# Issuing the first load of x as two transfers: 32 rows of x, then 224

## The chip, the core and the metric

The kernel runs on one core of one Trainium2 chip. A core has engines that run side by side and wait for each other through semaphores: TensorE (PE, matrix products into the accumulation memory PSUM; its weight loads are listed as PEld), VectorE (DVE), ScalarE (ACT), GpSimd (POOL) and SyncE (SP), which here only issues DMA transfers. All transfers run on the core's 16 DMA engines. The metric is the time of one execution on the device in microseconds (us). The kernel before takes 358.84 us, the median of three runs between 358.75 and 359.02 us.

## The reference

```python
batch, seq, hidden = 16, 512, 768          # x: 16 x 512 x 768, w_qkv: 768 x 2304, float32
qkv = np.matmul(x, w_qkv)
q, k, v = qkv[..., :768], qkv[..., 768:1536], qkv[..., 1536:]
return np.stack([q, k, v], axis=0)         # 3 x 16 x 512 x 768, float32
```

It is one matrix product: 8192 rows of x (25 MB) by 2304 columns of weights (7 MB), and the 75 MB result is stored as three blocks.

## The kernel before

The rows of x are worked through in 32 pairs of 128-row blocks; "pair p" is rows 256p to 256p + 255. The 2304 columns are cut into two groups of 1024 (number q = 0 and 1) and a rest of 256. In the long main part, each pair and column group is multiplied by a seven-product scheme (Strassen-like, with sums of quarter blocks of x, made by GpSimd or VectorE, and sums of quarter blocks of the weights, made once by VectorE). Pairs are read in 32-partition pieces there and turned by VectorE. The order of the instructions on every engine is the order of the program text; nothing reorders it.

The start is different, since no weights are there yet. Pairs 0 and 1 are multiplied plainly, in bf16, while the weights arrive. What matters for the change is all in this start:

- All loads of the start are issued by SP, in this order: pair 0 of x (`load_rows(0)`, L453, 768 KB), pair 1 of x (`load_rows(1)`, L456, 768 KB), six pieces of the first weight block of 256 KB each (`load_blocks(0, 0, 1)`, L457), two halves of the second weight block (768 KB each), and then pair 2 of x in eight pieces of 96 KB, with the weights of the rest between them.
- `load_rows` (L159) puts rows m and 128 + m of a pair into partition m of the tile xin: 128 partitions, two runs of 3072 bytes in each. It is one transfer of 256 runs.
- The first eight transfers are issued at once. From the ninth on, each transfer on SP waits for the landing of the one issued eight before it, because eight completion semaphores are used in turn.
- `busy(10)` (L538) gives PE ten products of a zero tile, with nothing to wait for but the zeroing of that tile.
- `cast_rows(0)` (L539) turns pair 0 into bf16: VectorE takes one half of the columns (L165), ScalarE the other (L166), for each of the two 128-row blocks. These instructions wait for the landing of pair 0.
- `turn_rows(0, ...)` (L540) has PE transpose pair 0, 12 transposes of 128x128 (L185); VectorE and ScalarE copy them back from PSUM into xb (L194, L192). Between the two kinds of copies stands `cast_rows(1)`, which waits for the landing of pair 1.
- VectorE then casts the first two weight pieces (L542 and L543, recorded as L476), and `turn_rows(1)` (L544) transposes pair 1.
- `block(0, 0, ...)` (L547) are the first real products, 24 of 128x512 at L496, weight piece by weight piece. In PE's order they stand behind the 12 transposes of pair 1.

Of the kernel before, what the change touches and what calls it, by code (L numbers as in the profile page):

```python
# [10 lines left out]
def kernel(  # L11
# [20 lines left out]
    nc = tc.nc  # L32
    P = 128
# [87 lines left out]
    xin, xf, xb, sr = {}, {}, {}, {}  # L121
# [34 lines left out]

    def load_rows(p):  # L159
        xin[p] = xin_pool.tile([P, 2, K], fp32, name="xin")  # L160
        rows = x_flat[p * 2 * P:(p + 1) * 2 * P, :]
        nc.sync.dma_start(xin[p][:], rows.rearrange("(r m) k -> m r k", m=P))  # L162

    def copy_halves(dst, src):
        nc.vector.tensor_copy(out=dst[0], in_=src[0])  # L165
# [284 lines left out]
    ND = 2  # L450
    zero = xb_pool.tile([P, CB], bf16, name="zero", tag="xb")
    nc.vector.memset(zero[:], 0.0)
    load_rows(0)  # L453
    nc.scalar.activation(tiny[:], zero[:, :1], ident)
    make_identity(nc, eye)
    load_rows(1)  # L456
    load_blocks(0, 0, 1)  # L457
    load_blocks(0, 1)
# [246 lines left out]
```

## Time and profile before

| what | value |
|---|---|
| median of three runs | 358.84 us |
| the profiled execution: its own time, its span | 358.81 us, 357.0 us |
| PE busy (matmul), share of the span | 350.6 us, 98% |
| VectorE, ScalarE, GpSimd busy | 74%, 52%, 50% |
| DMA: bytes moved, mean rate | 108.10 MB, 303 GB/s |
| issue of the first two loads of x on SP | 0.74 to 1.69 us |
| start of the casts of pair 0, of pair 1 | 4.97 us, 6.93 us |
| first real product on PE | 8.29 us |

The span is the time between the first and the last recorded event of the one profiled execution; 1.8 us of its own time lie outside it. Times in the profile count from the start of the span. A busy PE is not proof of a PE at its peak: the records overlap and their ends are modelled. How late PE gets its first real product, and whether it waits later, is read from the chain of waits and from the timeline.

The trace also holds a record of each DMA packet (start, duration, size; one packet is one contiguous run of a transfer here) and of each landing: every transfer counts its semaphore up 16 times, once for each DMA engine, and is complete with the sixteenth.

### The profile page before, as it was taken

What the parts mean: (1) busy time and instruction counts of PE and PEld (TensorE: products, weight loads), DVE (VectorE), ACT (ScalarE), POOL (GpSimd) and SP (SyncE); (2) the same over time, 40 slices, a digit from 0 to 9 for tenths busy, and PEclk for the clock granted to TensorE, in tenths of its full rate; (3) what the DMA queues carried; (4) which work ended last, traced back from release to release, by engine and by line L of the source; (5) the groups of instructions that cost most, each with busy time, mean ns of one, the idle gap of its engine ahead of it and who ended that gap; (6) DMA issues with size and microseconds to landing.
All of it is one profiled execution on the core that took longest, in us unless ns stands there. A gap on an engine that the chain in (4) does not pass through costs nothing.

```text
span 357.0 us, 5315 instructions
## 1 busy us (share of the span) xinstructions
PE 350.6 (98%) x1757; PEld 252.1 (71%) x1776; DVE 264.4 (74%) x310; ACT 185.0 (52%) x317; POOL 177.3 (50%) x184
## 2 busy tenths in 40 slices
PE   7999999999999999999999999999999999999996
PEld 3474677768677686877768677686877768677674
DVE  3789876796877869777695877869777695876743
ACT  4587754545454553645545454553645545454553
POOL 0031773376566453665535566353665535566320
PEclk9999999999999999999999999999999999999999
DMA  7997999999999898998979899698999979887497
GB/s 296 380 353 238 325 378 340 373 317 348 308 311 340 257 361 206 347 266 285 361 197 385 227 342 307 209 402 213 347 263 307 331 196 392 225 303 280 155 380 260
DMA packets 82075, 108.10 MB, mean 303 GB/s; under 512 B 4992, under 2 KB 62080, under 8 KB 82048
## 3 DMA queue, kind: packets, MB, share of 16 engines
q1 hardware_dynamic: 75088, 102.52, 85.7%
q10 hardware_dynamic: 6960, 5.24, 5.5%
q8 instruction: 14, 0.23, 0.3%
q14 instruction: 13, 0.11, 0.1%
HBM read 32.24 MB, written 75.50 MB: 302 GB/s over the span
## 4 chain that ended last, share of the span: by engine, by line
PE 74%; POOL 15%; DVE 6%; issue 3%; DMA 2%; ACT 0%; SPq 0%
PE ps L258 56%; PE ps L321 12%; PE ps L496 6%; DVE xf L155 6%; POOL xb L205 5%; POOL s L226 3%; POOL s L225 3%; POOL s L227 3%; DMA xin<-in_x_dram 2%; PE ps L185 0%; DVE o L304 0%; ACT xc L166 0%; SPq L162 0%; DVE orem L424 0%; ACT orem L423 0%
## 5 line engine op out<-in xcount | busy, mean ns | idle before, releaser
L258 PE MATMUL ps<-t,s 128*128 128x512 f32 x720 | 177.9, 395 | 0.0
L258 PEld LDWEIGHTS ps<-t,s 128*128 128x128 f32 x720 | 135.1, 188 | 29.5
L155 DVE STREAM_TRANSPOSE xf<-xin 128x768 f32<-128x768 f32 (+1 forms) x45 | 93.3, 2075 | 4.3 <-DMA xin<-in_x_dram 4.3
L258 PE MATMUL ps<-b,xb 128*128 128x512 bf16 x343 | 81.6, 379 | 1.1
L298 DVE TENSOR_TENSOR o<-o,ps 128x512 f32<-128x512 f32 x56 | 38.5, 688 | 50.7 <-ACT o L297 50.0
L205 POOL CAST xb<-xf 128x1536 bf16<-128x1536 f32 x28 | 41.1, 1467 | 56.9 <-DVE xf L155 54.8
L225 POOL TENSOR_TENSOR s<-xf 128x384 fp32r<-128x384 f32 x29 | 31.0, 1068 | 72.9 <-DVE xf L155 71.1
L258 PEld LDWEIGHTS <-xb 128*128 128x128 bf16 x360 | 33.9, 98 | 36.7 <-issue 3.9
L304 DVE TENSOR_TENSOR o<-o,ps 128x512 f32<-128x512 f32 x60 | 41.1, 687 | 20.5 <-PE ps L258 19.4
L297 ACT ACTIVATE o<-ps 128x512 f32<-128x512 f32 x56 | 33.5, 598 | 42.1 <-PE ps L258 42.1
L258 PE MATMUL ps<-b,s 128*128 128x512 f32 x180 | 50.6, 389 | 0.0
L301 ACT ACTIVATE o<-ps 128x512 f32<-128x512 f32 x60 | 35.9, 598 | 25.2 <-PE ps L258 22.8
L378 DVE TENSOR_TENSOR o<-o,ps 128x512 f32<-128x512 f32 x78 | 47.8, 680 | 0.0
L321 PE MATMUL ps<-w_rem,xb 128*128 128x256 bf16 x384 | 47.4, 273 | 0.0
L286 ACT ACTIVATE o<-ps 128x512 f32<-128x512 f32 x60 | 35.9, 599 | 19.4 <-PE ps L258 14.0
L321 PEld LDWEIGHTS <-xb 128*128 128x128 bf16 x384 | 37.3, 98 | 11.5 <-issue 0.5
L335 ACT ACTIVATE orem<-ps 128x512 f32<-128x512 f32 x31 | 18.5, 598 | 48.3 <-PE ps L321 34.0
L258 PEld LDWEIGHTS ps<-b,s 128*128 128x128 f32 x180 | 33.8, 188 | 7.0
L226 POOL TENSOR_TENSOR s<-s,xf 128x384 fp32r<-128x384 f32 x29 | 29.5, 1018 | 2.3
L227 POOL TENSOR_TENSOR s<-xf 128x384 fp32r<-128x384 f32 x29 | 29.4, 1015 | 0.0
L229 POOL TENSOR_TENSOR s<-xf,s 128x384 fp32r<-128x384 f32 x29 | 29.2, 1008 | 0.0
L382 ACT ACTIVATE o<-ps 128x512 f32<-128x512 f32 x26 | 15.5, 598 | 17.9 <-PE ps L258 17.3
(49 smaller groups left out, 161.2 us busy)
## 6 DMA issues: line engine op xcount, KB each, us to landing
out_dram<-o SPq DMA_DIRECT2D x60, 768.0 KB, 4.6
out_dram<-o SPq DMA_DIRECT2D x75, 256.0 KB, 3.8
xin<-in_x_dram SPq DMA_DIRECT2D x88, 192.0 KB, 5.6
out_dram<-orem SPq DMA_DIRECT2D x31, 256.0 KB, 2.2
xin<-in_x_dram ACTq DMA_DIRECT2D x24, 192.0 KB, 4.4
st<-in_w_qkv_dram SPq DMA_DIRECT2D x5, 768.0 KB, 7.9
xin<-in_x_dram SPq DMA_DIRECT2D x2, 768.0 KB, 4.9
st<-in_w_qkv_dram SPq DMA_DIRECT2D x6, 256.0 KB, 6.0
```

Source lines behind the costliest of these rows:

```text
L155: nc.vector.transpose(turned[:, g:g + n], rows[:, g:g + n])
L205: nc.gpsimd.tensor_copy(out=xb[p][:], in_=xf[p][:])
L225: 1: lambda g: g.tensor_tensor(s[:, 1], a21, a22, op=add),
L226: 2: lambda g: g.tensor_tensor(s[:, 2], s[:, 1], a11, op=sub),
L227: 3: lambda g: g.tensor_tensor(s[:, 3], a11, a21, op=sub),
L258: nc.tensor.matmul(ps[:], lhs[j], rhs[j], start=(start and j == 0), stop=(j == KH - 1), skip_group_check=True,)
L286: nc.scalar.activation(c12, u.x[:], ident)
L298: nc.vector.tensor_tensor(c22, c22, u.y[:], op=add)
L301: nc.scalar.activation(c21, u.x[:], ident)
L304: nc.vector.tensor_tensor(c12, c12, u.y[:], op=add)
L321: nc.tensor.matmul(ps, xb[p][:, j, r * P:(r + 1) * P], w_rem[j // KH][:, j % KH, :], start=(j == 0), stop=(j == KT - 1), skip_group_check= ...
L378: dve.tensor_tensor(c, c, u.z[:], op=add)
```

## The change

The helper `load_rows` gets a list of partition ranges and issues one transfer for each of them. Pair 0 of x is loaded with two ranges, partitions 0 to 15 and then 16 to 127. As each partition holds two rows, that is 32 rows (96 KB, 32 runs of 3072 bytes) and 224 rows (672 KB, 224 runs). Pair 1 is loaded as before, in one transfer. Nothing is changed on the engines that compute: the casts of pair 0 stand where they stood and now wait for two landings. SP issues one transfer more, ahead of all that follow.

```diff
-    def load_rows(p):
+    def load_rows(p, parts=(slice(0, P), )):
         xin[p] = xin_pool.tile([P, 2, K], fp32, name="xin")
         rows = x_flat[p * 2 * P:(p + 1) * 2 * P, :]
-        nc.sync.dma_start(xin[p][:], rows.rearrange("(r m) k -> m r k", m=P))
+        rows = rows.rearrange("(r m) k -> m r k", m=P)
+        for m in parts:
+            nc.sync.dma_start(xin[p][m], rows[m])
...
-    load_rows(0)
+    load_rows(0, (slice(0, 16), slice(16, P)))
     nc.scalar.activation(tiny[:], zero[:, :1], ident)
     make_identity(nc, eye)
     load_rows(1)
```

## The prediction

> **What bounds the kernel now.** I read the chain that ended last first, in its opening 20 us (start, length, what):
>
> ```profile
> 0.74 0.44 SPq L162
> 1.18 0.06 issue
> 1.24 5.67 DMA xin<-in_x_dram
> 6.91 0.02 issue
> 6.93 0.53 ACT xc L166
> 7.46 0.05 issue
> 7.51 0.95 PE ps L185 x12
> 8.46 2.82 PE ps L496 x13
> ```
>
> The run waits for pair 1 of x until 6.91 us, then goes through a cast and PE's twelve transposes into the first real products. Then I asked who PE waits for over the whole span:
>
> ```profile
> PE ps L469 <- DVE zero L452: 1.2, 1, 1.2
> PE ps L185 <- ACT xc L166: 0.6, 1, 0.6
> ```
>
> That is the whole list: after the cast of pair 1, PE waits for nobody up to its last product. So the start shifts the end one for one, and the question is only when pair 1, and the weights right behind it, land. The timeline (start, duration, idle time before and what ended it) shows how tightly these follow the loads:
>
> ```profile
> 0.74 0.95 SPq L162 DMA_DIRECT2D xin<-in_x_dram  x2
> 4.97 0.63 DVE L165 CAST xc<-xin 128x384 bf16<-128x384 f32 x2 [3.84 <-DMA xin<-in_x_dram]
> 6.12 0.77 DVE L194 COPY xb<-ps 128x384 bf16<-128x384 bf16 x2 [0.52 <-PE ps L185]
> 6.93 0.63 DVE L165 CAST xc<-xin 128x384 bf16<-128x384 f32 x2
> 8.26 0.43 DVE L476 CAST b<-st 128x512 bf16<-128x512 f32 x1 [0.27 <-DMA st<-in_w_qkv_dram]
> ```
>
> Last, the rate of the DMA engines in short stretches (last two columns: busy share, GB/s):
>
> ```profile
> 1.75:2.00 0.25, 0.25 (x2) 0.00 (x0) 0.00 (x0) 0.25 (x1) 0.00 (x0) 1.00 1.13 172
> 2.00:2.25 0.25, 0.25 (x2) 0.15 (x1) 0.00 (x0) 0.22 (x2) 0.00 (x0) 1.00 0.59 98
> 2.25:2.50 0.25, 0.25 (x2) 0.06 (x1) 0.00 (x0) 0.00 (x0) 0.00 (x0) 1.00 0.32 86
> 2.50:2.75 0.25, 0.25 (x2) 0.09 (x1) 0.00 (x0) 0.00 (x0) 0.00 (x0) 1.00 0.81 209
> 3.00:3.25 0.25, 0.25 (x2) 0.02 (x1) 0.00 (x0) 0.00 (x0) 0.00 (x0) 1.00 1.00 406
> 9.00:10.00 1.00, 1.00 (x6) 0.48 (x5) 0.93 (x3) 0.86 (x2) 0.00 (x0) 1.00 1.04 402
> 15.00:16.00 1.00, 1.00 (x6) 0.49 (x5) 1.00 (x3) 1.00 (x3) 0.00 (x0) 1.00 1.07 373
> 17.00:18.00 1.00, 1.00 (x6) 0.43 (x5) 0.77 (x2) 0.49 (x2) 0.69 (x1) 1.00 1.14 275
> 18.00:19.00 1.00, 1.00 (x8) 0.59 (x7) 0.38 (x1) 0.78 (x2) 1.00 (x2) 1.00 1.20 249
> ```
>
> The reader is to see three things. The first packet starts 1.1 us after SP begins the issue (1.84 against 0.74 us). For about 0.9 us the engines then crawl: the packet records show first packets of 0.12 to 0.59 us where later ones of the same 3072 bytes take 0.121 us. From 3.0 us the queue is full and moves 400 GB/s, so nothing but bytes in front of pair 1 sets its landing. And at 17 to 19 us the rate falls to 249: there the 32-partition pieces of pair 2 run one behind another.
>
> **The change, part by part.**
>
> *One transfer more to issue.* The issues of the first loads take 0.44 to 0.45 us on SP with 0.05 between, so every later issue moves about 0.45 us back. Pair 1's goes from 1.24 to about 1.65, its packets could start near 2.75, and in the run of before its turn comes only at about 4.1 us (the first landing of pair 0, 4.45, less some 0.35 from the last packet of an engine to its landing record): over 1 us of cover. Without that cover it would cost 0.45. The weights behind are covered by still more. The queue of semaphores shifts by one, and each transfer keeps its partner eight before; new is only that the sixth weight piece, issued at 4.37 before and about 4.8 now, waits for the small first part, which lands near 3.1. Behind it on SP stand the second weight block and pair 2, with over 4 us of queued data ahead of them. Cost 0.
>
> *The small first part starts earlier.* Issues of 32-partition pieces that had waited take 0.31 us at least, such of 128 partitions 0.34 to 0.38. A shorter issue puts the first packet earlier by 0.03 to 0.13; I take 0.08, nearest to the difference between these rows. Gain −0.08.
>
> *What the first part does in the slow start.* It gives each engine two packets. In the run of before, each engine got through two or three packets until about 2.7 us. The lower bound is a gain: if the crawl comes from the first touch alone and the large part's packets find the path open at about 2.3 us (its issue near 1.2 plus 1.1), up to 0.4 us of crawl is saved. The upper bound: the 32-partition pieces take 0.396 us each (the landing records of six in a row, 17.65 to 20.03), 248 GB/s; half as many partitions at half that rate are 98,304 bytes in 0.79 us, all of it behind the first latency of about 0.45, ending near 3.0, so +0.3. I take 0: 0.79 from 1.76 ends at 2.55, inside the crawl.
>
> The page "SBUF — State Buffer" of the Trainium skill (section "Door 1: The DMA port swizzle") has partitions 0 to 15 reach only 4 of 16 ports, at a measured 104 GB/s; an estimate by it is 0.95 us for this part, ending at 2.71, and the sum would rise by about 0.1. No run here shows 16 partitions alone.
>
> *What the large part does.* 112 partitions over 16 engines is 7 each, 14 packets. At the full-height row (0.121 us a packet) that is 1.69 us, and the two parts together cost no more than before: lower bound 0. The other bound is from the 32-partition pieces: eight packets an engine at 0.036 us (their best in the trace, mixed with other traffic) would be 0.288 us, and they take 0.396, a factor of 1.37. By that factor the large part takes 2.32 us, +0.63. Pieces that do not cover the whole height make engines wait for each other at the writing side; with 7 partitions to an engine instead of 8 the engines' shares no longer coincide with those of the full-height transfers, so I go by the height-cut row although 112 is nearer to 128 in number: being cut is what sets it apart. Worse than the factor is possible where one engine meets others at each step, up to +1.1. I take +0.63. The slowest engine carries the lag through pair 1 and all weights, as each engine works its list in order at one rate.
>
> *Two waits on the cast of pair 0.* One more semaphore instruction, 0.02 to 0.05 us as in the rows of that kind on VectorE and PE. VectorE ends the copies of pair 0 at 6.894, just ahead of pair 1's landing at 6.905, so of 0.05 some 0.04 shows at most if pair 1 lands on time; with both loads late alike the same. I take +0.02.
>
> Sum: −0.08 + 0 + 0.63 + 0.02 = +0.57 us. The profiled execution's own time was 358.81 (357.0 of span and 1.8 around it), 0.03 under the median, so 359.38 by it and 359.41 by the median; I say 359.4. Pair 1 would land near 7.47, and the first real product start near 8.86.
>
> **The rivals.**
>
> *Hidden anyway.* The large part runs at the full rate and the early start cancels the second wait: −0.08 + 0.02, 358.8. For it: 112 is almost 128; the whole load is 16 packets an engine either way. Against it: the 249 GB/s at 18 us. The page "DMA: Bandwidth & Descriptors" (section "Rules for kernel authors") says of two transfers to disjoint partition halves: "Don't bother — they serialize"; by that rule the time stays here or rises a little. No run here shows it for a load cut in two.
>
> *The warm start, faster.* The small part takes the crawl on itself while the large one is being issued, and the large one runs at 400 GB/s from 2.3 to 2.4 us. Pair 1 then lands 0.3 to 0.5 us earlier: 358.4. For it: the crawl costs about 0.6 us (221 KB moved up to 3.0 us, where 406 GB/s from 1.84 on would have moved 471), and by far the longest packets are each engine's first two. It decides if the crawl is tied to the time of the first touch and not to each engine's first packets of each transfer, and if the height-cut part isn't slowed. Against it: in the records the third packet of most engines starts only at 2.65 to 2.95, later than a start of the large part at 2.3 would help much.
>
> *The first part is itself the brake.* Its writes come after the first latency, and the large part meets the worse sharing: +0.3 and +0.63 to +1.1, 359.8 to 360.2. For it: 16 partitions are half of the row that runs at 248 GB/s. Against it: the crawl leaves room.
>
> **How the numbers follow.** Forecast (height-cut large part, 359.0 to 359.8): 0.50. Hidden anyway: 0.20. Warm start: 0.13. The brake: 0.17. About 0.2%, 0.72 us, is what a measurement of this kernel tells from no change. Faster than 358.12 takes a saving of the whole crawl: 0.03, out of the warm start. Slower than 359.56: a third of the forecast's chance and nearly all of the brake's, 0.33. The rest, 0.64, is within. The range from 358.45 to 360.0 leaves out about half of the warm start and half of the brake, 0.15 together.
>
> **What would show it.** Right: pair 1's cast starts at 7.3 to 7.7 on ACT, the first product about 1.36 later, the rate is 280 to 350 GB/s in 3 to 5 us, the first packet starts at 1.7 to 1.8, and PE still waits for nobody afterwards. Wrong: pair 1's cast at 6.9 or before with 400 GB/s from 2.5 on (warm start or hidden), or the cast of pair 0 waiting past 5.7 (the brake). A wait of SP on the small part's landing, or a slower PE clock after the longer gap before pair 1, would be a cause not in the sum.

## The result, and the profile after

The changed kernel takes 359.52 us, the median of 21 runs, beside 358.91 us for 21 runs of the kernel before: +0.61 us. The ratio is 1.0024, with a 95% interval from 1.0015 to 1.0033. The lowest runs differ by as much, 359.30 against 358.68. Five of the 21 lie apart, at 360.53 to 361.63 us, and the kernel before has no such run (its highest is 359.59); they come up again under "The runs over 360 us". The ratio here and below is close to that of the mean times, so runs that lie apart weigh in it more than in the medians. The profiled execution took 359.35 us, with a span of 357.6 us, 0.6 more than before.

Line numbers from the change on are 2 higher than before. The chain that ended last, in its first 20 us (start, length, what):

```profile
0.74 0.39 SPq L164
...
1.18 0.41 SPq L164
...
1.65 5.79 DMA xin<-in_x_dram
7.43 0.02 issue
7.46 0.53 ACT xc L168
7.99 0.11 issue
8.10 0.89 PE ps L187 x12
```

It is the same chain with one more issue on SP, and pair 1 of x is waited for until 7.43 us instead of 6.91. The loss is complete there: the cast that follows starts at 7.46 instead of 6.93 (+0.53), the first real product at 8.82 instead of 8.29 (+0.53). Whom PE waits for in the whole span is again a list with two entries:

```profile
PE ps L187 <- ACT xc L168: 1.3, 2, 0.9
PE ps L471 <- DVE zero L454: 1.2, 1, 1.2
```

So PE still waits for nobody after pair 1's cast; the wait for the casts has doubled (1.3 us in two places, where it was 0.6 in one), since the cast of pair 0 is now late as well. The timeline of the start (start, duration, idle time before and what ended it):

```profile
5.77 0.63 DVE L167 CAST xc<-xin 128x384 bf16<-128x384 f32 x2 [4.64 <-DMA xin<-in_x_dram]
6.91 0.77 DVE L196 COPY xb<-ps 128x384 bf16<-128x384 bf16 x2 [0.52 <-PE ps L187]
7.60 0.62 DVE L167 CAST xc<-xin 128x384 bf16<-128x384 f32 x2
8.82 1.46 PE L498 MATMUL ps<-b,xb 128*128 128x512 bf16 x6
```

Pair 0's cast starts 0.80 us later (5.77 for 4.97), pair 1's on VectorE 0.67 later, as it now stands right behind the late copies of pair 0. The rate of the DMA engines in stretches (the last two columns: busy share, GB/s) shows why:

```profile
1.75:2.00 0.25, 0.25 (x2) 0.00 (x0) 0.00 (x0) 0.25 (x1) 0.00 (x0) 1.00 0.96 295
...
2.50:2.75 0.25, 0.25 (x2) 0.09 (x1) 0.00 (x0) 0.00 (x0) 0.00 (x0) 1.00 0.48 61
2.75:3.00 0.25, 0.25 (x2) 0.13 (x1) 0.00 (x0) 0.00 (x0) 0.00 (x0) 1.00 0.32 37
3.00:3.25 0.25, 0.25 (x2) 0.02 (x1) 0.00 (x0) 0.00 (x0) 0.00 (x0) 1.00 0.72 221
4.50:5.00 0.50, 0.50 (x2) 0.15 (x1) 0.00 (x0) 0.00 (x0) 0.00 (x0) 1.00 0.94 289
```

There are two slow starts now. The small first part's 32 packets run from 1.77 to about 2.3 us, each in 0.12 to 0.23 us, at 295 GB/s in the first stretch; its landings come only at 2.88 to 3.20. The large part's first packets start at 2.26, take up to 0.8 us, and then the rate falls to 61 and 37 GB/s, in the very stretches in which the kernel before climbed from 209 to 406. The queue is full only from about 3.25 us, a quarter of a microsecond later than before, and then it moves 289 to 375 GB/s from 4.0 to 5.0 us with packets of 0.156 to 0.164 us (medians at 4.25 to 5.25), where 400 GB/s and 0.121 us were the rule before. The large part's landings, one for each DMA engine, come at 5.23 to 5.67 us, and pair 1's at 7.12 to 7.43 (before: 6.36 to 6.91).

So two things could carry the +0.53: packets that are slower because the part has 112 partitions instead of 128, and a slow start that comes a second time, some 0.4 us later (2.26 for 1.84). The experiments part them.

### The profile page after: what moved, and what is told of

Same layout as the page of the kernel before. It is cut to its first block, busy times and chain, and to the rows that moved or that the text cites. A ratio compares the mean times of both kernels' runs of the same rounds, so it can differ in the third digit from the quotient of the medians.

```text
span 357.6 us, 5318 instructions
## 1 busy us (share of the span) xinstructions
PE 350.5 (98%) x1757; PEld 252.1 (70%) x1776; DVE 264.1 (74%) x310; ACT 185.3 (52%) x317; POOL 177.3 (50%) x184
## 4 chain that ended last, share of the span: by engine, by line
PE 74%; POOL 15%; DVE 6%; issue 3%; DMA 2%; ACT 0%; SPq 0%
PE ps L260 56%; PE ps L323 12%; PE ps L498 6%; DVE xf L155 6%; POOL xb L207 5%; POOL s L228 3%; POOL s L227 3%; POOL s L229 3%; DMA xin<-in_x_dram 2%; PE ps L187 0%; SPq L164 0%; DVE o L306 0%; ACT xc L168 0%; DVE orem L426 0%; ACT orem L425 0%
```

## The experiments

Three theories run through them. A: the cut in height (partitions) slows the large part. B: the large part is issued one issue later and has a slow start of its own, whatever ran before it. C: PE's clock comes up late, or falls back, when PE has too little work in the gap before the data. Each kernel was timed in alternation with the kernel before; times are medians, with the number of runs, and "before" is the median of the same comparison. The comparisons ran on three chips: the two cuts at other places, the other order and the spare transfer on one; the tiny transfers, the changed kernel with twelve products and the row blocks on a second; the last three of "The runs over 360 us" on a third; the chip of the first comparison is not on record. From one execution to the next of the same kernel, the start of pair 1's cast differs by about 0.1 us: it is at 7.46 in the changed kernel's first profile and at 7.58 in its second.

### Where the 0.53 us come from

**Cut by columns instead of partitions.** Both parts have all 128 partitions: columns 0 to 95, then 96 to 767.

```diff
-    def load_rows(p, parts=(slice(0, P), )):
+    def load_rows(p, parts=(slice(0, K), )):
...
-            nc.sync.dma_start(xin[p][m], rows[m])
+            nc.sync.dma_start(xin[p][:, :, m], rows[:, :, m])
...
-    load_rows(0, (slice(0, 16), slice(16, P)))
+    load_rows(0, (slice(0, 96), slice(96, K)))
```

> Pair 0 of x in two transfers cut by columns: 96 columns (98,304 bytes, as many as the 32 rows had), then 672, each over all 128 partitions. The extra issue of the changed kernel is kept, the cut in height is gone. Theory A (the height-cut large part is slow on its way): the packets of the large part go at full pace again (2688-byte packets near 106 ns, none at 140 to 180), pair 1's cast starts at 6.9 to 7.0 us and the time is 358.8 to 359.0. Theory B (the large part, issued 0.45 us later, has a slow start of its own): the rate stays under 250 GB/s up to about 3.0 us and pair 1's cast starts at 7.2 to 7.3, time 359.1 to 359.3. If each holds in part, the rate tells how much: after, the cast is at 7.46.

Measured: 359.91 us (12 runs) beside 359.02, ratio 1.0025 (1.0014 to 1.0036); six runs lie over 360, so the median is far above the profiled execution (359.26 us). The rates of that one:

```profile
2.50:2.75 0.25, 0.25 (x2) 0.09 (x1) 0.00 (x0) 0.00 (x0) 0.00 (x0) 1.00 0.54 86
2.75:3.00 0.25, 0.25 (x2) 0.13 (x1) 0.00 (x0) 0.00 (x0) 0.00 (x0) 1.00 0.17 54
3.00:3.25 0.25, 0.25 (x2) 0.02 (x1) 0.00 (x0) 0.00 (x0) 0.00 (x0) 1.00 0.84 290
4.50:5.00 0.50, 0.50 (x3) 0.15 (x1) 0.00 (x0) 0.00 (x0) 0.00 (x0) 1.00 1.02 399
```

With the full height the steady rate is back (399 GB/s for 289), but the second slow start is there (86 and 54), and pair 1's cast starts at 7.35 us, +0.42. That A is worth the remaining 0.1 does not follow: it is no more than two executions differ, and pair 1's landings lie further apart here (6.67 to 7.33 us) than in the changed kernel (7.12 to 7.43). What A is worth is worked out from the rates below.

**A spare transfer first, then pair 0 whole.** The same 96 KB go to a spare buffer, and pair 0 is loaded in one transfer of full height. This moves 96 KB more, two packets an engine.

```diff
-    load_rows(0, (slice(0, 16), slice(16, P)))
+    spare = both[:16, 0, :2 * K].rearrange("p (r k) -> p r k", r=2)
+    nc.sync.dma_start(spare, x_flat[:2 * P, :].rearrange("(r m) k -> m r k", m=P)[:16])
+    load_rows(0)
```

> The 32 rows are loaded into a spare buffer that nothing reads before it is overwritten, and then pair 0 is loaded whole, in one transfer over all 128 partitions. The first transfer and the later issue of the second are those of the changed kernel, the height cut is gone, and 98,304 bytes are loaded in addition (two packets an engine, 0.24 us at full pace). Theory A: steady 400 GB/s from 2.9 us on as before, pair 1's cast at 6.9 to 7.1 us, time 358.8 to 359.0. Theory B: under 250 GB/s until about 3.0 to 3.2 us, then 400 at once; 32 packets an engine after that put pair 1's cast at 7.2 to 7.5, time 359.2 to 359.5.

Measured: 359.43 us (11 runs, one of them 361.10) beside 359.02, ratio 1.0015 (1.0006 to 1.0024). The rates of the profiled execution:

```profile
2.50:2.75 0.25, 0.25 (x2) 0.10 (x1) 0.00 (x0) 0.00 (x0) 0.00 (x0) 1.00 0.21 37
2.75:3.00 0.25, 0.25 (x2) 0.13 (x1) 0.00 (x0) 0.00 (x0) 0.00 (x0) 1.00 0.25 98
4.50:5.00 0.50, 0.50 (x2) 0.15 (x1) 0.00 (x0) 0.00 (x0) 0.00 (x0) 1.00 1.07 430
```

Pair 1's cast starts at 7.35 us, 0.11 earlier than in the changed kernel, although each engine has two packets of 0.121 us more to do, 0.24 us. By these two profiles the height cut costs about 0.35 us by itself; the changed kernel gets 0.24 of it back, as the small part's packets are a part of the load and not extra.

**A tiny transfer first.** The kernel before, with 8 KB (16 runs of 512 bytes, the last rows of x) read into a spare buffer ahead of pair 0. This is one issue more and almost no bytes.

```diff
+    nc.sync.dma_start(both[:16, 0, :P], x_flat[M - 16:M, :P])
     load_rows(0)
```

> A transfer of only 16 runs of 512 bytes (8 KB, from the last rows of x, into a spare buffer) is issued first, then pair 0 whole as before. Nothing is cut in height and no bytes to speak of are added: what is left is the later issue of pair 0 alone. Theory B (a large transfer brings its own slow start, so pair 0 gets going as much later as it is issued later): under 250 GB/s up to about 3.0 us, pair 1's cast 0.25 to 0.45 us later than before (7.2 to 7.35), time +0.25 to +0.45. Theory A (only the cut in height costs): cast at 6.9 to 7.0, time unchanged.

Measured: 359.35 us (11 runs, none over 359.5) beside 359.01, ratio 1.0010 (1.0001 to 1.0018). The rates of the profiled execution:

```profile
2.75:3.00 0.25, 0.25 (x2) 0.13 (x1) 0.00 (x0) 0.00 (x0) 0.00 (x0) 1.00 0.29 98
...
3.25:3.50 0.25, 0.25 (x2) 0.15 (x1) 0.00 (x0) 0.00 (x0) 0.00 (x0) 1.00 1.06 430
```

This is B alone, and it costs +0.34 us by the medians and +0.41 at the first product (8.70 us for 8.29). The small transfer at 1.77 us has warmed nothing for the load behind it: that load starts one issue later (its first packet at 2.27 us for 1.84) and goes through its slow start in full.

**The same tiny transfer, touching every 16th row of pair 0.** If the slow start belonged to the first access to these rows, this would take some of it away. The edit to the kernel with the tiny transfer:

```diff
-    nc.sync.dma_start(both[:16, 0, :P], x_flat[M - 16:M, :P])
+    nc.sync.dma_start(both[:16, 0, :P], x_flat[:2 * P, :].rearrange("(a b) k -> b a k", b=16)[0][:, :P])
```

> As the run with the tiny first transfer, but its 16 runs are the first 512 bytes of every sixteenth row of pair 0, so that the memory of pair 0 has been touched all over before pair 0 is loaded. If the slow start is the first touch of that memory, pair 0 goes at 300 GB/s or more by 2.5 to 2.75 us and pair 1's cast starts 0.3 us or more earlier than with the other tiny transfer (6.7 to 7.0). If it belongs to the start of a large transfer whatever its addresses, this run and the other are the same within 0.15 us.

Measured: 359.39 us (11 runs) beside 359.01, ratio 1.0010 (1.0002 to 1.0019), the same as without the touch. In the rates of its profiled execution

```profile
2.75:3.00 0.25, 0.25 (x2) 0.13 (x1) 0.00 (x0) 0.00 (x0) 0.00 (x0) 1.00 0.21 86
```

the slow start stands where it stood, and pair 1's cast starts no earlier (7.50 us, for 7.33 without the touch). A touch of every 16th row does not lift it; what makes it stays open.

**What each theory is worth in the changed kernel.** The rates over two longer stretches show it, for the kernel before, the changed one and the one with the tiny transfer from the last rows of x, in this order:

```profile
1.50:4.00 2.50, 2.50 (x7) 0.91 (x6) 0.00 (x0) 0.72 (x2) 0.00 (x0) 1.00 0.78 258
4.00:5.50 1.50, 1.49 (x4) 0.30 (x2) 0.53 (x2) 0.53 (x2) 0.00 (x0) 1.00 1.01 406
...
1.50:4.00 2.50, 2.50 (x7) 0.91 (x6) 0.00 (x0) 0.71 (x2) 0.00 (x0) 1.00 0.74 215
4.00:5.50 1.50, 1.40 (x4) 0.30 (x2) 0.00 (x0) 0.00 (x0) 0.00 (x0) 1.00 1.04 340
...
1.50:4.00 2.50, 2.50 (x7) 0.91 (x6) 0.00 (x0) 0.72 (x2) 0.00 (x0) 1.00 0.60 196
4.00:5.50 1.50, 1.50 (x4) 0.30 (x2) 0.16 (x1) 0.16 (x1) 0.00 (x0) 1.00 1.02 410
```

Up to 4.0 us, before the packets turn slow, the changed kernel moves 43 GB/s less than the kernel before, 108 KB, which take 0.26 us at 406 GB/s: that is B. From 4.0 to 5.5 us, where the packets of the cut part are slow, it moves 66 GB/s less, 0.24 us: that is A. The two are about equal, and together they are nearly the 0.53 us at pair 1's cast. In a second profile of the changed kernel (208 and 320 GB/s in the same stretches) they are 0.31 and 0.32 us. The kernel with the tiny transfer loses 0.38 us in the first stretch and nothing in the second. It loses more in the first because it has next to nothing to move while the large load is being issued; the changed kernel has the small part.

The landings show the cut in height a second way. Each engine closes its share of a transfer with a packet of 4 bytes, and its landing follows. With the full height it follows 0.32 to 0.34 us later, on average over the engines (the first loads of the kernel before and of the column cut). For the cut parts of the changed kernel it is 0.85 us for the 16 partitions and 0.65 for the 112, and for the two halves of 64 (below) 0.98 and 0.94. So the data of a cut part land well after its packets are over.

**The order of the parts, and their sizes.** First the large part (112 partitions) and then the small one; and two halves of 64.

```diff
-    load_rows(0, (slice(0, 16), slice(16, P)))
+    load_rows(0, (slice(0, 112), slice(112, P)))
```

> The same two parts the other way round: 224 rows (partitions 0 to 111) first, then 32 rows. The large part is issued at 0.74 us as the whole load was before, the height cut stays. Theory A: the rate is under 380 GB/s in 3 to 5 us, pair 1's cast starts at 7.2 to 7.6 us, time 359.1 to 359.6. Theory B: the slow start is that of the kernel before (over 300 GB/s from 2.75 us on), pair 1's cast at 6.9 to 7.0, time 358.8 to 359.0.

Measured: 361.11 us (6 runs, 359.87 to 361.88) beside 359.02, ratio 1.0051 (1.0036 to 1.0066). The rates of the profiled execution (361.35 us):

```profile
2.75:3.00 0.25, 0.25 (x2) 0.13 (x1) 0.00 (x0) 0.00 (x0) 0.00 (x0) 1.00 0.94 369
3.50:4.00 0.50, 0.50 (x3) 0.15 (x1) 0.00 (x0) 0.00 (x0) 0.00 (x0) 1.00 1.01 258
5.00:5.50 0.50, 0.05 (x1) 0.00 (x0) 0.00 (x0) 0.00 (x0) 0.00 (x0) 1.00 1.02 154
```

The queue is nearly full from 2.75 us (369 GB/s, where the changed kernel has 37), so the second slow start is gone, as B says. But then the rate falls to 258 and 154 GB/s with packets of 0.18 to 0.31 us (medians of quarter microseconds in these two stretches), and pair 1's cast starts at 8.39 us, +1.46, later than either theory had it. In this order the slow packets are by far the larger loss; why they are slower than with the small part first stays open. A slower PE clock comes on top (below).

```diff
-    load_rows(0, (slice(0, 16), slice(16, P)))
+    load_rows(0, (slice(0, 64), slice(64, P)))
```

> Pair 0 cut in the middle: partitions 0 to 63, then 64 to 127, eight packets an engine in each part. Theory A (a transfer that covers only part of the height makes the engines wait for each other): far worse than after, packets near 230 ns, 200 to 300 GB/s in 3 to 6 us, pair 1's cast at 8 to 8.6 us, time 360 to 360.7. Theory B: the first part is long enough to hide the second one's start, so no loss: cast at 6.9 to 7.0 us, time 358.8 to 359.0.

Measured: 361.50 us (6 runs) beside 359.02, ratio 1.0077 (1.0062 to 1.0093); the profiled execution took 362.62. Its rates:

```profile
3.50:4.00 0.50, 0.50 (x2) 0.15 (x1) 0.00 (x0) 0.00 (x0) 0.00 (x0) 1.00 1.05 215
5.00:5.50 0.50, 0.50 (x2) 0.00 (x0) 0.00 (x0) 0.00 (x0) 0.00 (x0) 1.00 1.01 203
```

and two steps of its chain:

```profile
0.74 0.72 SPq L164
7.35 1.48 PE ps L187 x12
```

The halves move 203 to 215 GB/s, about half of the full height, and the loss is larger than A had it. The "SBUF — State Buffer" page of the Trainium skill, section "Door 1: The DMA port swizzle", gives 196 GB/s for partitions 0 to 63, measured on 1 MiB, and about 218 as the limit; here the trace agrees. Two more losses come on top: the first issue takes 0.72 us instead of 0.44, and the transposes 1.48 us instead of 0.95, as PE's clock is still low: they start every 0.107 us, where the kernel before mostly has 0.056.

### The runs over 360 us

**Two zero products more in the changed kernel.** PE has work for some 0.4 us longer before pair 0 lands.

```diff
-    busy(10)
+    busy(12)
```

> The changed kernel with twelve products of the zero tile ahead of the first transposes instead of ten, so that PE is busy through most of the gap that the later pair 0 leaves (5.4 to 6.3 us). Theory C (the runs of the changed kernel at 360.5 to 361.6 us, 6 of 21, are those in which PE's clock falls back to half, or comes up later, for want of work in the gap): the lowest time stays at 359.3, and runs over 360.2 become rarer than 1 in 10. Against it: if these runs have another cause, 2 to 4 in 10 stay over 360.2.

Measured: 359.68 us (11 runs, highest 359.98) beside 359.01, ratio 1.0016 (1.0008 to 1.0025). No run lies over 360, where the changed kernel has 5 of 21 in the first series and 3 of 5 in a second (below). If 8 of the 37 runs were high by chance, none of these 11 would be among them in about 4 of 100 draws. The 11 were taken on another chip than the second series, without the changed kernel beside them, so the chip is a rival that no run here excludes. The filler does not help the bulk of the runs: the median of the 16 other runs of the changed kernel is 359.42.

**Two zero products fewer in the kernel before.** No load is changed at all.

```diff
-    busy(10)
+    busy(8)
```

> The kernel before, with eight zero products ahead of the first transposes instead of ten: all loads are those of before, but PE has a gap of about 0.9 us ahead of the transposes of pair 0 (4.64 to 5.55), as long as the one in the changed kernel (5.41 to 6.33). Theory C (the slow tail comes from PE's clock, for want of work in that gap): 2 to 4 runs in 10 lie 1 us or more above the lowest, the others at 358.8 to 359.2 like before. If the tail comes from the transfers, no run does, and the times are those of before.

Measured: 359.97 us (12 runs) beside 359.01, ratio 1.0016 (1.0005 to 1.0027). The 12 runs fall into two groups, five at 358.70 to 359.05 and seven at 359.90 to 360.38. The timeline of the profiled execution, one of the seven (360.15 us):

```profile
5.62 1.48 PE L185 MATMUL ps<-eye,xc 128*128 128x128 bf16 x12 [0.83 <-ACT xc L166]
6.89 0.94 ACT L166 ACTIVATE xc<-xin 128x384 bf16<-128x384 f32 x2 [0.91 <-DMA xin<-in_x_dram]
7.91 1.46 PE L185 MATMUL ps<-eye,xc 128*128 128x128 bf16 x12
```

The counterpart in the kernel before:

```profile
5.55 0.95 PE L185 MATMUL ps<-eye,xc 128*128 128x128 bf16 x12
```

The loads are on time (pair 1's cast at 6.89), but the transposes run at half speed, one every 0.107 us instead of mostly 0.056. The trace's record of the granted clock begins, with the full clock, only at 10.18 us, where it begins at 5.22 in the kernel before; of the time ahead of it the record says nothing. That is theory C shown for this start: with less filler and the same loads, seven of twelve runs, more than the 2 to 4 in 10 that were expected, are about 1.3 us longer, and the clock comes up late in the one of them that was profiled. The profile of the kernel with the large part first shows the other form (last three columns: granted clock, DMA busy share, GB/s):

```profile
5.00:7.00 2.00, 0.05 (x1) 0.00 (x0) 0.37 (x2) 0.38 (x1) 0.00 (x0) 1.00 0.98 270
7.75:9.00 1.25, 1.25 (x8) 0.60 (x7) 0.92 (x4) 0.61 (x2) 0.00 (x0) 0.50 1.05 405
9.00:11.16 2.16, 2.16 (x15) 1.58 (x15) 1.84 (x7) 1.63 (x5) 0.00 (x0) 0.50 1.06 408
11.16:12.00 0.84, 0.84 (x5) 0.39 (x4) 0.84 (x3) 0.43 (x1) 0.00 (x0) 1.00 1.04 402
```

PE idles for 2.15 us (5.05 to 7.20), and the clock falls to half from 7.75 to 11.16, for 3.41 us. "TensorE: Matmul & The Clock Gate" in the Trainium skill, Part 1, has the clock decided in free-running windows of 3.413 us. The trace agrees: the stretches at full clock last 351.573 us in the kernel before and in the changed one and 348.159 us in the one with eight products, which is 103 and 102 times 3.413. The same page ("Why this matters for your kernels") warns of gaps of PE over about 3 us; here 2.15 us were enough.

**The column cut with 12 products.**

```diff
-    def load_rows(p, parts=(slice(0, P), )):
+    def load_rows(p, parts=(slice(0, K), )):
...
-            nc.sync.dma_start(xin[p][m], rows[m])
+            nc.sync.dma_start(xin[p][:, :, m], rows[:, :, m])
...
-    load_rows(0, (slice(0, 16), slice(16, P)))
+    load_rows(0, (slice(0, 96), slice(96, K)))
...
-    busy(10)
+    busy(12)
```

> The cut by columns, with twelve zero products instead of ten. Its transfers had 6 of 12 runs 0.8 us or more above the lowest. Theory C: at most 1 in 10 now; lowest time unchanged at 359.2. If the transfers make the tail, 3 to 6 in 10 as without the added products.

Measured: 359.45 us (12 runs) beside 359.01, ratio 1.0022 (1.0012 to 1.0032), with four runs over 360. The median is lower than with ten products, on another chip, but four high runs are more than C allows, and the profiled execution is one of them (360.16 us). Its clock came up on time, at 5.03. Its chain is another:

```profile
2.75 6.20 DMA st<-in_w_qkv_dram
8.96 10.00 DMA str<-in_w_qkv_dram
19.01 1.22 POOL w_rem L562
20.28 2.45 PE ps L323 x21
```

Two of the 16 DMA engines are late: pair 1 landed on them at 7.47 and 7.62 us, on the rest by 7.15. The lag went on through the weights and grew on the way: the weights of the last 256 columns landed at 18.96 us, where 14 engines were done by 17.56, and PE had to wait for their cast until 20.28. Why it grew is not settled. So for the column cut there is a second cause of high runs, in the transfers, and C alone is not enough.

**The changed kernel once more**, unchanged, to catch one of its high runs in a profile.

> The changed kernel once more, beside the other two on the same chip, to have its tail there: 6 of 21 runs lay over 360.2 us in the first measurement. Expected: lowest 359.3, and 2 to 4 in 10 over 360.2, whatever theory holds; it is the standard for the two others and for the run with twelve zero products.

Measured: 360.28 us (5 runs, 359.50 to 360.87) beside 359.01, ratio 1.0035 (1.0023 to 1.0047); three of five are high. The profiled execution was not one of them: 359.50 us, first product at 8.95, full clock from 6.04. The high runs of the changed kernel itself were seen in no profile. That they are C's is argued, not shown. Three of the five in the first series have a mean granted clock of 0.995, the value of the profiled run with the large part first; half the clock for 3.41 us is a loss of about 1.7 us, and these three lie 1.6 to 2.2 us above the median of the 16. And no run with two more products was high. The other two of the five, and the three here, have 0.999 or 1.0. So have the seven high runs with eight products, of which the profiled one had its clock up late, so this value speaks neither for C nor against it; a lagging engine, as in the column cut, may have a share.

### A version meant to be faster

**Both pairs in two transfers by row block, full height**, so that the first 128 rows can be cast while the others land; the first weight pieces are multiplied with all four blocks from the start.

```diff
-    def load_rows(p):
+    def load_rows(p, parts=(slice(0, 1), slice(1, 2))):
...
-        nc.sync.dma_start(xin[p][:], rows.rearrange("(r m) k -> m r k", m=P))
+        rows = rows.rearrange("(r m) k -> m r k", m=P)
+        for m in parts:
+            nc.sync.dma_start(xin[p][:, m], rows[:, m])
...
-    singles = [((0, ), (0, 1)), ((1, ), (0, 1)), ((0, 1), (2, 3))]
-    singles += [((j, ), range(4)) for j in range(2, KT)]
+    singles = [((j, ), range(4)) for j in range(KT)]
```

> Pairs 0 and 1 each in two transfers by block of 128 rows (full height, one run of 3072 bytes per partition), so that the casts of a block wait for its half alone, and the first weight piece multiplied with all four blocks before the second (no other change; all bytes and products are as before). Theories A and B together: no height cut, and the first half (8 packets an engine) covers the issue and start of the second, so pair 1 lands no later than before (6.85 to 7.0 us). The cast of its first block is over earlier, and the first real product starts at 7.95 to 8.15 instead of 8.29 us: time 0.1 to 0.3 us under before. If every transfer's start costs anyway, pair 1 lands 0.2 us or more later and the time is not under before's.

Measured: 361.50 us (five runs, 360.23 to 362.41; a sixth took 2076 us, which nothing here explains) beside 359.01, ratio 1.0063 (1.0046 to 1.0080). The first cast starts early, at 3.80 us, but the transfers then stall; the rates of the profiled execution:

```profile
4.50:5.00 0.50, 0.50 (x5) 0.29 (x4) 0.26 (x1) 0.26 (x1) 0.00 (x0) 1.00 0.64 252
5.00:5.50 0.50, 0.50 (x10) 0.46 (x9) 0.14 (x2) 0.27 (x1) 0.00 (x0) 1.00 0.66 141
5.50:6.00 0.50, 0.50 (x8) 0.30 (x6) 0.42 (x2) 0.00 (x0) 0.00 (x0) 1.00 0.66 147
```

The engines are busy for 0.64 to 0.66 only, at 141 to 252 GB/s, with single packets of up to 0.74 us among those of the usual 0.121, and pair 1 lands at 8.67. The cause of this stall was not settled. No version tried beats the kernel before.

## Why the prediction was right, and where its sum was not

The total was right: 359.4 was forecast, and 359.52 measured; +0.57 was the sum, and +0.61 the difference of the medians (+0.53 at the first product of the profiled execution). What it said would be seen was seen: pair 1's cast at 7.46 (7.3 to 7.7 was the forecast), the first product 1.36 us later at 8.82, the first packet at 1.77, no wait of PE afterwards. The rate of 280 to 350 GB/s in 3 to 5 us holds only at the end of that stretch (289 from 4.5 to 5.0; 418 from 3.5 to 4.0). And one sign that was named for being wrong did show: pair 0's cast waited past 5.7 us, until 5.77. It was to stand for the small part as a brake. The kernel with the tiny transfer has that cast at 5.34, so 0.37 of the 0.80 us are the late start of the large part, and the rest goes with its cut in height, the slow packets and the late landings. The terms, too, were not what they seemed:

- **One transfer more to issue, "Cost 0".** This step failed. The cover it named, over 1 us, is pair 1's, and that was right: pair 1 was queued in time. The large part of pair 0 stands behind the added issue too, and it has no cover: nothing but the small part is queued in front of it. Its first packets start at 2.26 instead of 1.84, and its slow start comes after that. The tiny transfer, which adds the issue and next to nothing else, measures it: +0.34 us by the medians, +0.41 at the first product. In the changed kernel, where the small part moves meanwhile, it is 0.26 us by the rates (0.31 in the second profile).
- **The small part starts earlier, −0.08.** Its issue took 0.39 us instead of 0.44, and its first packet came 0.07 earlier. The size was right, but nobody profits: the load is complete with the large part.
- **The small part in the slow start, 0.** No cost of its own shows, as forecast: with 96 KB more to move, the spare transfer puts pair 1's cast at 7.35 us, the tiny one at 7.33. It is as slow as was weighed, though not in its packets, which take about 0.5 us: its last landing is at 3.20 (near 3.1 was said), and that less the usual 0.34 is 1.1 us after its first packet, beside the 0.79 and 0.95 of the two estimates. But the reading behind the 0, one crawl for the whole load in which two packets an engine fit, was wrong: the large part crawled anew.
- **The large part's height cut, +0.63 by a factor of 1.37.** The slowing is there, and the size was too large. The packets take 0.156 to 0.164 us instead of 0.121 at the end of the load, a factor of 1.3, but only at the end: 0.24 us by the rates (0.32 in the second profile), about 0.35 against the spare transfer. The reason given for it, that engines wait for each other at the writing side, fits the late landings of every cut part and the halves at half the rate, but no run tests it by itself.
- **Two waits on the cast, +0.02.** Not to be told apart from the rest.

So the sum came out because a term set to 0 that is about 0.3 here made up for one of 0.63 that is about 0.3. That the two errors cancelled was luck.

Of the rivals, "the warm start" hung on whether the slow start is tied to the first touch or to "each engine's first packets of each transfer". The rates at 2.5 to 3.0 us (61 and 37 GB/s) decide against it, and the two tiny transfers and the spare one repeat it. "Hidden anyway" fell with the same rows: even the kernel that adds only an issue is 0.34 us slower. "The first part is itself the brake" is right that the small part is slow to land and that pair 0's cast waits past 5.7. But it holds nothing up by that: the column cut, whose small part lands with the usual delay, moves no more up to 4.0 us (210 GB/s from 1.5 us on, 215 in the changed kernel), and the time stayed under that rival's 359.8.

The slower PE clock, named as a cause outside the sum, most likely makes at least some of the high runs. Without the five, the median of the other 16 is 359.42, +0.51 over before; the five lift the ratio above what the profiled execution shows.

In the expectations written before the runs, the high runs of the changed kernel are counted too many by one; over 360.2 us there are 5 of 21.

## What to carry to other kernels

A small head split off from the first load delays its bulk by one issue, and the bulk goes through a slow start of its own; when you look for the cover of an added issue, begin with the very next transfer, not with the ones that have a full queue in front of them. No cut of this load paid: one that keeps all partitions in each part held the full rate in the column cut (399 GB/s) but not in the row blocks, and neither was faster than the whole load. Filler work that holds PE's clock up should reach until the data land: two zero products fewer, with all loads as they were, made seven of twelve runs about 1.3 us longer.

## What was not expected of the hardware

- The slow start belongs here to the first large load, not to the kernel's first packets: after 8 KB or 96 KB had gone ahead, that load still had 0.5 us at 37 to 123 GB/s (2.5 to 3.0 us, where the kernel before has 209 and 319), even where every 16th of its rows had been read just before.
- The issues on SP of the two halves of 64 partitions took 0.72 and 0.60 us, and that of the whole pair 1 behind them 0.59. Those of 16, 112 and 128 partitions in the other kernels took 0.39 to 0.46, without an order by partitions: the same 16 took 0.39 us as the first issue and 0.45 as the second. The reason is open.
- The same 112 and 16 partitions cost 1.46 us at pair 1's cast with the large part first, and 0.53 with the small part first.
- Two zero products of about 0.4 us each, taken away from a filler off the critical path, made seven of twelve runs about 1.3 us longer.
